# Hybrid decoder layer on one core: two seams rewritten, and divided products placed by what PE has just done

## The chip, the core and the metric

The kernel runs on one core of one Trainium2 chip. The metric is the device time of one execution in microseconds (us), lower is better. The kernel before took 1909.48 us, the median of three runs (1909.34 to 1909.83).

## The reference

One decoder layer over a residual stream h of 256 rows by 2048 columns, all in f32:

```python
h = h + 0.5 * rms_norm(swiglu_ffn(rms_norm(h, g1), w_gu, w_down), p1)      # FFN1, d_ff = 5632
u = rms_norm(h, g2);  z = u @ w_in                                           # 2048 x 5120
a, g, q, k, v = split(z, [1024, 2048, 3072, 4096])
conv = silu(layer_norm(causal_depthwise_conv31(a * sigmoid(g))))
attn = causal_attention(rope(q), rope(k), v)       # 8 heads of 128; one block of 256 holds the sequence
h = h + rms_norm(concat(conv, attn) @ w_out, p2)
c = cross_attention(rms_norm(h, g3), rms_norm(mem, gm))   # 4 heads of 128, mem is 256 x 2048
h = h + rms_norm(c @ w_o, p3)
h = h + 0.5 * rms_norm(swiglu_ffn(rms_norm(h, g4), w_gu2, w_down2), p4)     # FFN2
```

where `swiglu_ffn(x) = (silu(x @ gate) * (x @ up)) @ down`, and rms_norm divides a row by the root of its mean square and multiplies by a gain.

## The kernel before

**Products.** Every f32 operand is split in two f32r parts, hi and lo, and a product is the sum of hi·hi, hi·lo and lo·hi. A weight tile is 128 partitions x 1024 columns (512 KB). It is loaded on SP's DMA queue into one of four `raw` buffers; ACT makes its hi (L183 where the norm's gain is multiplied in, L181 where not), DVE its lo (L199, L197). Each tile then gives PE 24 products of 256 columns. In `proj_T` (L443: gate and up, input projection, q, k) the weights stand still and a tile of activations moves; in `proj` (L457: down, v, `w_out`, x_o) the weights move. Activations lie in `chunk` tiles (`ck` and `cf` in the rows) of 512 columns, results in eight PSUM banks (`ps`).

**Order of the work.** Tiles are numbered as PE takes them. FFN1: 22 groups of gate and up with 8 tiles each (0 to 175), then down in two halves of 44 tiles (176 to 263). A boundary of residual updates, transposes (L340) and splits follows, in which PE is given products for the memory's k and v. Mixing: groups of the GLU, q, k and v, then the attention and, on DVE and POOL, the convolution's taps and its layer norm, then `w_out`. Cross-attention: q, attention, x_o (its 192 products with two activation chunks as operands come in two parts, first rows t = 0, then t = 1). FFN2 is FFN1 again.

**What runs beside.** `Weights.ahead()` issues loads and splits some tiles ahead. `Background` holds the small work (norms, gates, taps, transposes) in lanes: `add` puts a piece in, `cut` ends what one tile may take, and `step()` runs once per tile. The rows x are wanted as transposed chunks, 4 of them, put among the weights at tiles `X_AT` of the first group. A norm is four pairs of squares, a root, a diagonal, a broadcast on PE (L406) and a copy.

**Divided products.** `HALVED = (0, 4, 8)` names products of a tile that are given to PE as two of 128 columns. Before, they stand at fixed tiles: `(g, u) in ((1, 1), (2, 1))` of gate and up, `(hf, n) in ((0, 1), (0, 5))` of down, and `u == 1` of each group that is transposed in mixing.

**The start and the seam.** `Weights.start()` (L125 to L148) loads the first x chunk and the first weight tile by halves, behind one load of small vectors (L261). The seam before FFN2 is written out by hand behind the products of x_o: the transposes of t = 0, squares, gains and hi/lo of t = 0, then the last square of t = 1, the root (L496), reciprocal (L498), update (L501), transposes (L340), hi (L348), lo (L351), and the products of FFN2.

Of the kernel before, what the change touches and what calls it, by code (L numbers as in the profile page):

```python
# [33 lines left out]
X_AT = [0, 1, 3, 5]  # L34
# [12 lines left out]
class Background:  # L47


    def __init__(self):  # L50
        self.lanes = [deque(), deque()]
        self.lane = 0
        self.dve = deque()
        self.pool = deque()
        self.rate = (STEP_DVE, STEP_ACT, STEP_POOL)
        self.credit = [0.0, 0.0, 0.0]

    def add(self, fn, dve=0.0, act=0.0, pool=0.0):
        self.lanes[self.lane].append((fn, dve, act, pool))
# [8 lines left out]
    def step(self):  # L68
        self.credit = [min(c + d, d) for c, d in zip(self.credit, self.rate)]
        for lane in self.lanes:  # L70
            while lane:
                p = lane.popleft()
                if p is None:
                    break
                p[0]()
                self.spend(*p[1:])
# [23 lines left out]
class Weights:  # L100
# [10 lines left out]
    def add(self, src, gains=(None,), key=None, rows=False, loads=1):  # L111
        self.entries.append((src, gains, key, rows, loads))

    def load(self, upto):
        while self.n_raw < min(upto + 1, len(self.entries)):
            t = self.pool.tile([P, 1024], F32, name="raw", bufs=RAW)
            src, loads = self.entries[self.n_raw][0], self.entries[self.n_raw][4]
            n = 1024 // loads
            for e in range(loads):
                self.nc.sync.dma_start(t[:, e * n:(e + 1) * n], src[:, e * n:(e + 1) * n])  # L120
            self.raw[self.n_raw] = t
            self.n_raw += 1

    def start(self):

        for i in range(2):
            self.raw[i] = self.pool.tile([P, 1024], F32, name="raw", bufs=RAW)
        for i, e in ((0, 0), (1, 0), (1, 1), (0, 1)):
            c = slice(e * 512, (e + 1) * 512)
            self.nc.sync.dma_start(self.raw[i][:, c], self.entries[i][0][:, c])  # L130
        key = self.entries[0][2]
        self.chunks[key] = c = self.chunk()
        self.hi[key], self.lo[key] = c[:, :, 0, :], c[:, :, 1, :]
        self.hi[1] = self.pool.tile([P, 1024], F32R, name="hi", bufs=HI)
        self.lo[1] = self.pool.tile([P, 1024], F32R, name="lo", bufs=LO)
        for i, e in ((0, 0), (1, 0), (1, 1), (0, 1)):
            k = i if i else key
            src, hi, g = list(self.parts(i, self.hi[k]))[e]
            lo = list(self.parts(i, self.lo[k]))[e][1]
            if g is None:  # L140
                self.nc.scalar.activation(hi, src, AF.Copy)
                self.nc.vector.tensor_tensor(lo, src, hi.bitcast(F32), ALU.subtract)
            else:
                self.nc.scalar.activation(hi, src, AF.Copy, scale=g)  # L144
# [3 lines left out]
        self.n_raw = self.n_hi = self.n_lo = 2  # L148

    def parts(self, i, whole):  # L150

        _, gains, _, rows, _ = self.entries[i]
# [12 lines left out]
    def split_hi(self, upto):  # L165
        while self.n_hi < min(upto + 1, len(self.entries)):
            i = self.n_hi
            self.load(i)
            _, _, key, rows, _ = self.entries[i]
# [58 lines left out]
def layer_kernel(ctx: ExitStack, tc: tile.TileContext, x, mem, eye, consts, smalls, post_g, xt, memt,  # L228
# [32 lines left out]
    nc.sync.dma_start(sm[:, 0:S_CW], smalls[:, 0:S_CW])  # L261
# [3 lines left out]
    ones = cp.tile([P, P], F32, name="ones")  # L265
    nc.vector.memset(ones, 1.0)
# [6 lines left out]
    def add_ffn(gu, down, gain, extra):  # L273
        for g in range(2 * NG):
            for u in range(8):
                extra(-1, 8 * g + u)
                W.add(gu[g, u], [gain + 2 * u, gain + 2 * u + 1], loads=2 if len(W.entries) == 1 else 1)
# [11 lines left out]
    def first_extra(hf, k):  # L289
        kv_extra(0, hf, k, KV_AT1)  # L290
        if hf == -1 and k in X_AT:
            c = X_AT.index(k)
            W.add(xt[c], [None] * (2 if c == 0 else 1), ("x", c), True, 2 if c == 0 else 1)
# [4 lines left out]
    add_ffn(f1_gu, f1_down, S_G1, first_extra)  # L298
# [18 lines left out]
    add_ffn(f2_gu, f2_down, S_G2, lambda hf, k: None)  # L317

    def step(mm, k):
        W.ahead()  # L320
        hi, lo = W.take()
        mm(k, hi, lo)
        bg.step()
# [29 lines left out]
    class Rows:  # L353
# [10 lines left out]
        def tr(self, t, c):  # L364
            if self.xT[c] is None:
                self.xT[c] = chunk()
            self.ps[t, c] = transposes(self.src(t, c))

# [52 lines left out]
        def queue_norm(self, done=0):  # L421
# [25 lines left out]
    def proj(pss, first, last, hi, lo, xk, t, n0=0, halved=()):  # L447
# [3 lines left out]
        for n, ps in enumerate(pss):  # L451
            for o in (0, 256):
# [11 lines left out]
    class Post:  # L464


        def __init__(self, row, factor):
# [4 lines left out]
            self.ssq = [scal(4) for _ in range(2)]  # L472
# [14 lines left out]
        def early(self, t):  # L487

            s1 = scal()
            nc.vector.reduce_sum(s1, self.ssq[t][:, 0:3], axis=AX.X)  # L490
# [3 lines left out]
        def rstd(self, t):  # L494
            s2 = scal()
            nc.scalar.activation(s2, self.ssq[t][:, 3:4], AF.Sqrt, bias=self.bias, scale=self.factor / D)  # L496
            self.rs[t] = scal()
            nc.vector.reciprocal(self.rs[t], s2)  # L498

# [4 lines left out]
    def down(nk, lhs, post, hook=None, tail=TAIL, keep=False, order=None):  # L504

        order = order or range(nk)
        for hf in range(2):
# [3 lines left out]
            def mm(n, hi, lo):  # L511
# [36 lines left out]
    def boundary(post, last, rows, fillers):  # L548
# [36 lines left out]
        queue_rest(post, rows)  # L585

    def queue_rest(post, rows, early=False):
# [5 lines left out]
        def turns(c):  # L593
            for t in range(1 if early else 0, 2):
                bg.add(lambda t=t: rows.tr(t, c))
# [48 lines left out]
    def gate_up(rows):  # L644
        hT = []
        for g in range(2 * NG):
            pss = [bank() for _ in range(2)]

            def mm(u, hi, lo):
                for e in range(2):  # L650
                    k = 2 * u + e
                    proj_T(regions_of(pss), k == 0, k == KT - 1, hi[:, e * 512:], lo[:, e * 512:], rows.x(k),
                           g == k == 0, HALVED if e == 0 and (g, u) in ((1, 1), (2, 1)) else ())

            for u in range(8):
                step(mm, u)
            if g % 2 == 0:
                hT.append(chunk())
            c = slice(2 * (g % 2), 2 * (g % 2) + 2)
            queue_gate(pss[0], pss[1], rows, hT[-1][:, c, 0, :], hT[-1][:, c, 1, :])  # L660
# [56 lines left out]
    nc.sync.dma_start(sm[:, S_CW:S_W], smalls[:, S_CW:S_W])  # L717
    for c in range(4):
# [11 lines left out]
    hT = gate_up(rows)  # L730
# [49 lines left out]
    def in_group(hook=None):  # L780
        pss = [bank() for _ in range(2)]

        def mm(u, hi, lo):
            for e in range(2):
                k = 2 * u + e
                proj_T(regions_of(pss), k == 0, k == KT - 1, hi[:, e * 512:], lo[:, e * 512:], rows.x(k), False,
                       HALVED if u == 1 and e == 0 else ())
# [122 lines left out]
    def queue_heads(heads):  # L910
        stages = [attn_stages(hh) for hh in heads]
        for n in range(len(stages) + 7):
            for i in range(len(stages)):
                if 0 <= n - i < 8:
                    fn, d, a = stages[i][n - i]
                    bg.add(fn, dve=d, act=a)
            bg.cut()

    def queue_ln():
# [62 lines left out]
        bg.add(means)  # L982
# [7 lines left out]
        bg.add(squares)  # L990
# [26 lines left out]
    def v_group(c, hook):  # L1017
# [3 lines left out]
        def mm(u, hi, lo):  # L1021
            for e in range(2):
                k = 2 * u + e
                for t in range(2):
                    proj([vps[t]], k == 0, k == KT - 1, hi[:, e * 512:], lo[:, e * 512:], rows.x(k), t)
# [46 lines left out]
    def mm_q(u, hi, lo):  # L1072
        for e in range(2):
            k = 2 * u + e
            proj_T(regions_of(qps), k == 0, k == KT - 1, hi[:, e * 512:], lo[:, e * 512:], rows.x(k))
# [38 lines left out]
    for n in range(XH + 4):  # L1114
        for i in range(XH):
            if 0 <= n - i < 5:
                fn, d, a = xs[i][n - i]
                bg.add(fn, dve=d, act=a)
# [81 lines left out]
    bg.add(lambda: rows.tr(1, 1))  # L1200
# [4 lines left out]
    hT = gate_up(rows)  # L1205
# [106 lines left out]
```

## Time and profile before

| | |
|---|---|
| median of three runs | 1909.48 us |
| the profiled execution's own time | 1908.69 us |
| its span | 1906.9 us |
| PE busy | 1885.5 us, 99% |
| DVE, ACT, POOL busy | 62%, 55%, 11% |
| read from memory | 365.61 MB, 193 GB/s over the span |

PE is the TensorE's matmuls, PEld its weight loads, DVE, ACT and POOL the vector, scalar and GpSimd engines, SP the queue that issues most transfers. The span is what the profiler saw, from the first instruction to the last; the execution's own time is 1.8 us longer. A matmul's end is modelled, so paces are read from starts: in rows of the form "start, busy, engine, line" the second number is the time from the first start to the last end of a run of like instructions. The share of 99% says that PE hardly ever waits; it says nothing on how fast it goes while busy.

### The profile page before, as it was taken

To read this page: it belongs to the slowest core of one execution; us is meant where nothing else is said; L and a number is where in the kernel's file an instruction comes from. 1 tells how busy PE (TensorE), PEld (TensorE's weight loads), DVE (VectorE), ACT (ScalarE), POOL (GpSimd) and SP (SyncE) were. 2 spreads that over 40 slices of the span, in tenths; PEclk is the share of its full clock that TensorE was granted. 3 is DMA by queue.
4 is the path that set the end of the run, shared out by engine and by line. 5 is a ranking of instruction groups with operands and counts; after the bars stand their busy time and mean duration, and the time that the engine had idled before them with its cause. 6 is when DMAs were issued, how large, how long until landed. Compare 5 with 4: busy or idle time off the path is not lost.

```text
span 1906.9 us, 39744 instructions
## 1 busy us (share of the span) xinstructions
PE 1885.5 (99%) x16436; PEld 1880.9 (99%) x16436; DVE 1182.6 (62%) x1611; ACT 1049.7 (55%) x1627; POOL 205.8 (11%) x182
## 2 busy tenths in 40 slices
PE   8999999999999999999999999999999999999998
PEld 8999999999999999999999999999999999999998
DVE  5656665666544457898886675666666666644444
ACT  6655555555444556687675575555555555533433
POOL 0000000000000000598420000000000000000000
PEclk9999999999999999999999999999999999999999
DMA  8556565555655775555555573555565555655554
GB/s 297 190 193 197 191 198 191 198 190 198 210 196 192 244 247 171 182 184 173 177 183 183 182 229 101 183 197 192 195 194 194 195 193 196 214 191 197 192 195 144
DMA packets 102133, 370.28 MB, mean 194 GB/s; under 512 B 11456, under 2 KB 11712, under 8 KB 101184
## 3 DMA queue, kind: packets, MB, share of 16 engines
q1 hardware_dynamic: 100944, 361.00, 57.2%
q10 hardware_dynamic: 1008, 6.75, 1.1%
q8 instruction: 128, 2.10, 0.5%
q14 instruction: 53, 0.43, 0.1%
HBM read 365.61 MB, written 2.10 MB: 193 GB/s over the span
## 4 chain that ended last, share of the span: by engine, by line
PE 95%; DMA 1%; DVE 1%; POOL 1%; ACT 1%; issue 0%; SPq 0%; DVEq 0%; POOLq 0%; ACTq 0%
PE ps L443 60%; PE ps L457 32%; POOL cv L778 1%; DMA raw<-in_f_gu_dram 1%; DMA raw<-in_f_down_dram 1%; PE ps L340 0%; PE ps L1133 0%; PE ps L1131 0%; PE ps L1132 0%; ACT hi L181 0%; DVE lo L197 0%; POOL cf L947 0%; PE ps L869 0%; PE ps L1153 0%; PE ps L1091 0%
## 5 line engine op out<-in xcount | busy, mean ns | idle before, releaser
L443 PE MATMUL ps<-ck,hi 128*128 128x256 f32 x6808 | 1166.7, 277 | 8.2 <-ACT hi L144 6.9
L443 PEld LDWEIGHTS ps<-ck,hi 128*128 128x128 f32 x6808 | 1027.3, 188 | 9.2 <-ACT hi L144 6.9
L443 PE MATMUL ps<-ck,lo 128*128 128x256 f32 x3404 | 938.9, 277 | 1.5 <-DVE lo L197 1.2
L199 DVE SCALAR_TENSOR_TENSOR lo<-raw,sm,hi 128x512 fp32r<-128x512 f32 x718 | 517.5, 762 | 356.7 <-issue 337.0
L183 ACT ACTIVATE hi<-raw,sm 128x512 fp32r<-128x512 f32 x718 | 479.7, 717 | 373.1 <-PE ps L443 231.1
L443 PEld LDWEIGHTS ps<-ck,lo 128*128 128x128 f32 x3404 | 638.2, 188 | 2.2 <-DVE lo L197 1.6
L457 PE MATMUL ps<-hi,ck 128*128 128x256 f32 x3596 | 616.4, 277 | 0.0
L197 DVE TENSOR_TENSOR lo<-raw,hi 128x1024 fp32r<-128x1024 f32 x296 | 373.1, 1261 | 288.4 <-PE ps L457 228.8
L457 PEld LDWEIGHTS ps<-hi,ck 128*128 128x128 f32 x3596 | 542.9, 188 | 0.4
L457 PE MATMUL ps<-lo,ck 128*128 128x256 f32 (+1 forms) x1798 | 496.6, 277 | 0.3 <-DVE lo L197 0.3
L181 ACT ACTIVATE hi<-raw 128x1024 fp32r<-128x1024 f32 x296 | 313.0, 1059 | 312.8 <-PE ps L457 251.5
L457 PEld LDWEIGHTS ps<-lo,ck 128*128 128x128 f32 x1798 | 337.1, 188 | 0.6 <-DVE lo L197 0.5
L629 POOL TENSOR_TENSOR tmp<-tmp,rb 128x512 f32<-128x512 f32 x44 | 57.9, 1316 | 1128.4 <-ACT tmp L628 1128.4
L778 POOL TENSOR_TENSOR cv<-cv,cf 128x255 f32<-128x255 f32 (+14 forms) x120 | 123.3, 1029 | 306.4 <-ACT cf L777 298.3
L777 ACT ACTIVATE cf<-yv,cf 128x255 f32<-128x255 f32 (+14 forms) x120 | 56.7, 490 | 25.7 <-POOL cv L778 25.4
L768 DVE SCALAR_TENSOR_TENSOR ps<-yv,cf,ps 128x254 f32<-128x254 f32 (+28 forms) x116 | 54.4, 469 | 2.4
L348 ACT ACTIVATE ck<-tmp 128x512 fp32r<-128x512 f32 x44 | 27.8, 632 | 46.1 <-DVE tmp L632 46.1
L345 ACT ACTIVATE tmp<-ps 128x512 f32<-128x512 f32 x32 | 19.1, 598 | 33.0 <-PE ps L457 28.5
L482 DVE TENSOR_TENSOR fg<-ps,cf 128x512 f32<-128x512 f32 x32 | 21.3, 685 | 15.8 <-ACT tmp L345 15.8
L625 DVE TENSOR_TENSOR tmp<-ps,rb 128x512 f32<-128x512 f32 x44 | 30.1, 685 | 0.1
L351 DVE TENSOR_TENSOR ck<-tmp,ck 128x512 fp32r<-128x512 f32 x44 | 30.1, 685 | 0.0
L632 DVE TENSOR_TENSOR tmp<-tmp,ps 128x512 f32<-128x512 f32 x44 | 29.6, 674 | 0.0
(132 smaller groups left out, 649.6 us busy)
## 6 DMA issues: line engine op xcount, KB each, us to landing
raw<-in_f_gu_dram SPq DMA_DIRECT2D x351, 512.0 KB, 4.2
raw<-in_f_down_dram SPq DMA_DIRECT2D x176, 512.0 KB, 4.2
raw<-in_w_in_dram SPq DMA_DIRECT2D x80, 512.0 KB, 3.3
raw<-in_w_out_dram SPq DMA_DIRECT2D x32, 512.0 KB, 3.5
cf<-in_post_g_dram ACTq DMA_DIRECT2D x4, 1024.0 KB, 6.5
raw<-in_x_k_dram SPq DMA_DIRECT2D x8, 512.0 KB, 4.5
raw<-in_x_q_dram SPq DMA_DIRECT2D x8, 512.0 KB, 4.0
raw<-in_x_o_dram SPq DMA_DIRECT2D x8, 512.0 KB, 4.3
```

Of the source, the lines that this page charges most:

```text
L181: self.nc.scalar.activation(dst, src, AF.Copy)
L183: self.nc.scalar.activation(dst, src, AF.Copy, scale=g)
L197: self.nc.vector.tensor_tensor(dst, src, hi.bitcast(F32), ALU.subtract)
L199: self.nc.vector.scalar_tensor_tensor(dst, src, g, hi.bitcast(F32), ALU.mult, ALU.subtract)
L351: nc.vector.tensor_tensor(lo, src, hi.bitcast(F32), ALU.subtract)
L443: nc.tensor.matmul(ps[:, o + a:o + a + w], (hi, hi, lo)[i][:, j * P:(j + 1) * P], xk[:, i % 2, a:a + w], start=first and o == 0 and i == 0 ...
L457: nc.tensor.matmul(ps[:, a:a + d], xs[i], w[:, c:c + d], start=first and a == 0 and i == 0, stop=last and i == 2, skip_group_check=True)
L625: nc.vector.tensor_tensor(two(box[0]), two(G), bc2(rows.rb), ALU.mult)
L629: nc.gpsimd.tensor_tensor(two(box[0]), two(box[0]), bc2(rows.rb), ALU.mult)
L768: nc.vector.scalar_tensor_tensor(o, yv[:, ct, :S - s], w, a[:, s:], ALU.mult, ALU.add)
L777: nc.scalar.activation(pr[:, :S - s], yv[:, ct, :S - s], AF.Copy, scale=w)
L778: nc.gpsimd.tensor_tensor(cv[:, ct, s:], cv[:, ct, s:], pr[:, :S - s], ALU.add)
```

## The change

- **Start.** The small vectors are loaded on ACT's queue. The first transfers are a quarter of the x chunk, half a weight tile, a quarter, half, two whole weight tiles and then the rest of the x chunk. Nine f32 products of a tile of ones with itself are given to PE first. The first three groups of gate and up of FFN1 run side by side (`gu_order`, `SIDE = 3`): for each u one tile of each of the three groups; `X_AT` moves with them. The loads of the residual rows are four cuts later.
- **Divided products.** `Background.settle()` decides for each tile. Pieces that give PE other work than these products are marked `pe=True`; when one has run, or at the start of a half of down, behind a boundary, or behind the seam, `mixed` is set. The next tile but a group's first (`k` not 0) is divided if `mixed` is set and no marked piece stands in the next five cuts of any lane. It now holds for v groups and q too, and x_o has one fixed divided product set.
- **Norms.** One more cut stands between the root and the diagonal of each norm, so that everything behind it comes a tile later.
- **The seam before FFN2.** The last bank of x_o is computed in two sides of 256 columns; the last square is done in two halves; the update, transposes, hi and lo of the first chunk of t = 1 go by halves, with ACT's other work behind them.

```diff
-X_AT = [0, 1, 3, 5]
+X_AT = [0, 4, 10, 16]
+SIDE = 3
...
+    def settle(self, ahead=5):
+        if not self.mixed:
+            return False
+        for lane in self.lanes:
+            n = 0
+            for p in lane:
+                n += p is None
+                if n >= ahead:
+                    break
+                if p is not None and p[4]:
+                    return False
+        self.mixed = False
+        return True
...
     def start(self):
-        for i, e in ((0, 0), (1, 0), (1, 1), (0, 1)):
-            c = slice(e * 512, (e + 1) * 512)
+        x0, w0 = (0, slice(0, 256), slice(0, 1)), (1, slice(0, 512), None)
+        x1, w1 = (0, slice(256, 512), slice(1, 2)), (1, slice(512, 1024), None)
+        x2 = (0, slice(512, 1024), slice(2, 4))
...
+        for p in (x0, w0, x1, w1):
+            fetch(*p)
+        self.n_raw = 2
+        self.load(3)
+        fetch(*x2)
+        for p in (x0, w0, x1, w1):
+            split(*p)
+        self.n_hi = self.n_lo = 2
+        self.split_lo(2)
+        split(*x2)
...
-    nc.sync.dma_start(sm[:, 0:S_CW], smalls[:, 0:S_CW])
+    nc.scalar.dma_start(sm[:, 0:S_CW], smalls[:, 0:S_CW])
+    ones = cp.tile([P, P], F32, name="ones")
+    nc.vector.memset(ones, 1.0)
+    wps = bank()
+    for _ in range(9):
+        nc.tensor.matmul(wps[:, 0:P], ones, ones, start=True, stop=True)
...
+    def gu_order(side):
+        return [(g, u) for u in range(8) for g in range(side)] + [(g, u) for g in range(side, 2 * NG) for u in range(8)]
...
     def step(mm, k):
         W.ahead()
         hi, lo = W.take()
+        halved[:] = HALVED if k and bg.settle() else ()
         mm(k, hi, lo)
+        halved[:] = ()
         bg.step()
...
             bg.add(self.rstd, dve=0.4, act=0.4)
+            bg.cut()
             bg.add(self.diag, dve=0.4)
             bg.cut()
-            bg.add(self.bcast)
+            bg.add(self.bcast, pe=True)
...
-                    at = HALVED if t == 0 and (hf, n) in ((0, 1), (0, 5)) else ()
-                    proj(pss[t], n == 0, n == nk - 1, hi, lo, lhs(order[n]), t, 0, at)
+                    proj(pss[t], n == 0, n == nk - 1, hi, lo, lhs(order[n]), t, 0, halved if t == 0 else ())
+            bg.mixed = True
...
-                           g == k == 0, HALVED if e == 0 and (g, u) in ((1, 1), (2, 1)) else ())
+                       u == 0 and g < side and (side > 1 or e == 0), halved if e == 0 else ())
...
+    for _ in range(4):
+        bg.cut()
     for c in range(4):
         for t in range(2):
             bg.add(lambda t=t, c=c: nc.sync.dma_start(h_rows(t, c), x[t * P:(t + 1) * P, c * 512:(c + 1) * 512]))
...
-            proj(ps0[2 * hf:2 * hf + 2], k == 0, k == XH - 1, *wo[4 * hf + k], oT[:, k], 0)
+            proj(ps0[2 * hf:2 * hf + 2], k == 0, k == XH - 1, *wo[4 * hf + k], oT[:, k], 0, 0,
+                 HALVED if (hf, k) == (0, 1) else ())
...
-        for k in range(XH):
-            proj([ps1[c]], k == 0, k == XH - 1, *wo[4 * (c // 2) + k], oT[:, k], 1, c % 2)
+        for sides in [(0, 256)] if c < 3 else [(0,), (256,)]:
+            for k in range(XH):
+                proj([ps1[c]], k == 0, k == XH - 1, *wo[4 * (c // 2) + k], oT[:, k], 1, c % 2, (), sides)
...
-    post.early(1)
-    for c in range(2):
-        rows.hi(0, c)
-        rows.lo(0, c)
-    post.square(1, 3, ps1[3])
+    post.square_half(1, 0, ps1[3])
+    post.early(1, 4)
+    post.square_half(1, 1, ps1[3])
     post.rstd(1)
-    post.update(1, 0)
+    rows.hi(0, 0)
+    for e in range(2):
+        post.update_half(1, 0, e)
+        rows.tr_half(1, 0, e)
+    rows.hi_half(1, 0, 0)
+    rows.lo_half(0, 0, 0)
+    rows.lo_half(1, 0, 0)
+    rows.hi_half(1, 0, 1)
+    rows.lo_half(0, 0, 1)
+    rows.lo_half(1, 0, 1)
+    rows.hi(0, 1)
     post.gain(1, 3, ps1[3])
-    rows.tr(1, 0)
-    rows.hi(1, 0)
-    rows.lo(1, 0)
+    rows.lo(0, 1)
     post.update(1, 1)
```

**The order of instructions at three places.** SP's queue from its first transfer, before:

```order
L261 DMA sm<-in_smalls_dram 128x80
L130 DMA raw<-in_xt_dram 128x512
L130 DMA raw<-in_f_gu_dram 128x512 x2
L130 DMA raw<-in_xt_dram 128x512
L120 DMA raw<-in_xt_dram 128x1024
L120 DMA raw<-in_f_gu_dram 128x1024 x2
L120 DMA raw<-in_xt_dram 128x1024
L120 DMA raw<-in_f_gu_dram 128x1024
L716 DMA ident<-in_eye_dram 128x128
```

The same stretch after (`in_xt` is x transposed, `in_f_gu` the weights of gate and up):

```order
L153 DMA raw<-in_xt_dram 128x256
L153 DMA raw<-in_f_gu_dram 128x512
L153 DMA raw<-in_xt_dram 128x256
L153 DMA raw<-in_f_gu_dram 128x512
L140 DMA raw<-in_f_gu_dram 128x1024 x2
L153 DMA raw<-in_xt_dram 128x512
L140 DMA raw<-in_f_gu_dram 128x1024
L140 DMA raw<-in_xt_dram 128x1024
L140 DMA raw<-in_f_gu_dram 128x1024
L797 DMA ident<-in_eye_dram 128x128
```

The small vectors are gone from the head of this queue, a quarter of x stands ahead of the first half tile of weights, and the second whole transfer of x comes behind three whole weight tiles rather than ahead of them. DVE at the seam before FFN2, before:

```order
L482 TENSOR_TENSOR fg<-ps,cf 128x512 x3
L490 TENSOR_REDUCE scal_14397<-scal_14099 128x1
L492 TENSOR_SCALAR scal_14399<-scal_14397 128x1
L351 TENSOR_TENSOR ck<-ps,ck 128x4x128 x2
L498 RECIPROCAL scal_14409<-scal_14407 128x1
L501 SCALAR_TENSOR_TENSOR h<-fg,scal_14409,h 128x512
L482 TENSOR_TENSOR fg<-ps,cf 128x512
L351 TENSOR_TENSOR ck<-ps,ck 128x4x128
L501 SCALAR_TENSOR_TENSOR h<-fg,scal_14409,h 128x512
```

And after (L482/L550 is the gain, L351/L399 the lo, L501/L575/L579 the update):

```order
L550 TENSOR_TENSOR fg<-ps,cf 128x512 x3
L562 TENSOR_REDUCE scal_14403<-scal_14100 128x1
L565 TENSOR_SCALAR scal_14405<-scal_14403 128x1
L571 RECIPROCAL scal_14411<-scal_14409 128x1
L575 SCALAR_TENSOR_TENSOR h<-fg,scal_14411,h 128x256 x2
L399 TENSOR_TENSOR ck<-ps,ck 128x2x128 x4
L550 TENSOR_TENSOR fg<-ps,cf 128x512
L399 TENSOR_TENSOR ck<-ps,ck 128x4x128
L579 SCALAR_TENSOR_TENSOR h<-fg,scal_14411,h 128x512
```

The two lo's of t = 0 stood ahead of the reciprocal and now stand behind the update, which has become two halves. PE from the end of the cross-attention to FFN2, before:

```order
L1104 MATMUL ps<-ident,cf 128x128 x4
L1153 MATMUL ps<-cf 128x256 x8
L457 MATMUL ps<-ck 128x256 x192
L340 MATMUL ps<-ident,h 128x128 x20
L443 MATMUL ps<-ck,hi 128x256 x8
```

And after:

```order
L1238 MATMUL ps<-cf 128x256 x8
L525 MATMUL ps<-ck 128x256 x12
L525 MATMUL ps<-ck 128x128 x2
L525 MATMUL ps<-ck 128x256 x3
L525 MATMUL ps<-ck 128x128 x2
L525 MATMUL ps<-ck 128x256 x3
L525 MATMUL ps<-ck 128x128 x2
L525 MATMUL ps<-ck 128x256 x171
L388 MATMUL ps<-ident,h 128x128 x16
L424 MATMUL ps<-ident,h 128x128 x4
```

Three of x_o's 192 products are now two each; the last four transposes have become two pairs (L424).

## Rows read from the trace of the kernel before

**Rows 1.** The page: busy us of an engine, share, instructions.

```profile
PE 1885.5 (99%) x16436; PEld 1880.9 (99%) x16436; DVE 1182.6 (62%) x1611; ACT 1049.7 (55%) x1627; POOL 205.8 (11%) x182
```

**Rows 2.** PE's waits: waiting line, releaser; total us, times, longest.

```profile
PE ps L443 <- ACT hi L144: 6.9, 1, 6.9
PE ps L340 <- DVE h L501: 1.8, 1, 1.8
PE ps L443 <- DVE lo L197: 1.2, 2, 1.0
```

**Rows 3.** The chain that ended last: start us, us, what.

```profile
52.90 438.49 PE ps L443 x3867
...
661.34 45.99 PE ps L457 x406
...
736.48 2.87 PE ps L443 x24
...
759.17 8.49 PE ps L443 x72
...
1147.37 23.03 PE ps L457 x192
```

**Rows 4.** Timeline of PE, a divided tile: start us, us, engine, line.

```profile
35.62 0.51 PE L443 MATMUL ps<-ck,hi 128*128 128x128 f32 x3
...
37.23 0.28 PE L443 MATMUL ps<-ck,lo 128*128 128x256 f32 x1
```

**Rows 5.** Timeline of PE, the first products and the stall at 20 us.

```profile
6.89 2.08 PE L443 MATMUL ps<-ck,hi 128*128 128x256 f32 x8 [6.89 <-ACT hi L144]
...
10.63 0.28 PE L443 MATMUL ps<-ck,lo 128*128 128x256 f32 x1
...
19.93 0.28 PE L443 MATMUL ps<-ck,lo 128*128 128x256 f32 x1
...
21.84 0.40 PE L443 MATMUL ps<-ck,hi 128*128 128x256 f32 x2
```

**Rows 6.** Windows: busy us of five engines; granted clock; DMA share; GB/s.

```profile
6.89:10.47 3.58, 3.58 (x16) 3.58 (x17) 2.71 (x4) 2.73 (x4) 0.00 (x0) 1.00 0.83 310
10.00:20.00 10.00, 10.00 (x84) 9.95 (x82) 6.27 (x8) 4.90 (x7) 0.00 (x0) 1.00 1.00 333
```

**Rows 7.** The chain of the first 60 us.

```profile
1.64 4.39 DMA raw<-in_f_gu_dram
...
6.12 0.73 ACT hi L144
...
13.33 6.62 DMA raw<-in_f_gu_dram
...
52.47 0.43 PE ps L406 x2
```

**Rows 8.** Timeline of SP's queue: the first issue.

```profile
0.74 0.38 SPq L261 DMA_DIRECT2D sm<-in_smalls_dram  x1
```

**Rows 9.** Timeline of the seam before FFN2.

```profile
1170.24 1.91 PE L340 MATMUL ps<-ident,h 128*128 128x128 f32 x16
...
1171.84 0.60 ACT L345 ACTIVATE tmp<-ps 128x512 f32<-128x512 f32 x1
...
1173.09 0.75 DVE L501 SCALAR_TENSOR_TENSOR h<-fg,scal,h 128x512 f32<-128x512 f32 x1
...
1173.99 0.63 PE L340 MATMUL ps<-ident,h 128*128 128x128 f32 x4 [1.85 <-DVE h L501]
...
1175.31 1.47 PE L443 MATMUL ps<-ck,hi 128*128 128x256 f32 x8 [0.69 <-ACT ck L348]
...
1176.61 0.63 PE L443 MATMUL ps<-ck,lo 128*128 128x256 f32 x4
```

**Rows 10.** The chain in mixing: where it leaves PE and comes back.

```profile
840.10 0.56 DVE tmp L801
...
869.68 1.48 DVE lo L197
```

More of the change, by code (lines that the diff above doesn't have):

```diff
@@ L109, in __init__, with add @@
         self.limit = None
-    def add(self, src, gains=(None,), key=None, rows=False, loads=1):
-        self.entries.append((src, gains, key, rows, loads))
+    def add(self, src, gains=(None,), key=None, rows=False):
+        self.entries.append((src, gains, key, rows))
     def load(self, upto):
@@ L116, in load @@
             t = self.pool.tile([P, 1024], F32, name="raw", bufs=RAW)
[L117 to L120, printed above, removed]
+            self.nc.sync.dma_start(t, self.entries[self.n_raw][0])
             self.raw[self.n_raw] = t
@@ L168, in split_hi @@
             self.load(i)
-            _, _, key, rows, _ = self.entries[i]
+            _, _, key, rows = self.entries[i]
             if rows:
@@ L271, in layer_kernel, with add_ffn @@
     W = Weights(nc, wp, chunk, sm)
[L273 to L277, printed above, removed]
+    def gu_order(side):
+        return [(g, u) for u in range(8) for g in range(side)] + [(g, u) for g in range(side, 2 * NG) for u in range(8)]
+    halved = []
+    def add_ffn(gu, down, gain, extra, side):
+        for n, (g, u) in enumerate(gu_order(side)):
+            extra(-1, n)
+            W.add(gu[g, u], [gain + 2 * u, gain + 2 * u + 1])
         for hf in range(2):
@@ L292, in first_extra @@
             c = X_AT.index(k)
-            W.add(xt[c], [None] * (2 if c == 0 else 1), ("x", c), True, 2 if c == 0 else 1)
+            W.add(xt[c], key=("x", c), rows=True)
         if hf == 1 and k in MEM_AT:
@@ L316, in layer_kernel @@
             W.add(x_o[o // 4, o % 4], key=("o", o))
[L317 removed]
+    add_ffn(f2_gu, f2_down, S_G2, lambda hf, k: None, 1)
     def step(mm, k):
@@ L367, in tr, with tr_half, hi_half, lo_half @@
             self.ps[t, c] = transposes(self.src(t, c))
+        def tr_half(self, t, c, e):
+            if self.xT[c] is None:
+                self.xT[c] = chunk()
+            if (t, c) not in self.ps:
+                self.ps[t, c] = bank().rearrange("p (k s) -> p k s", k=4)
+            for k in (2 * e, 2 * e + 1):
+                nc.tensor.transpose(self.ps[t, c][:, k], self.src(t, c)[:, k * P:(k + 1) * P], ident)
+        def hi_half(self, t, c, e):
+            k = slice(2 * e, 2 * e + 2)
+            make_hi(self.part(t, c, 0)[:, k], self.ps[t, c][:, k])
+        def lo_half(self, t, c, e):
+            k = slice(2 * e, 2 * e + 2)
+            make_lo(self.part(t, c, 1)[:, k], self.ps[t, c][:, k], self.part(t, c, 0)[:, k])
+            if e == 1:
+                self.ps.pop((t, c))
         def part(self, t, c, e):
@@ L445, in proj_T, with proj @@
                                  skip_group_check=True)
-    def proj(pss, first, last, hi, lo, xk, t, n0=0, halved=()):
+    def proj(pss, first, last, hi, lo, xk, t, n0=0, halved=(), sides=(0, 256)):
         xs = [xk[:, f, t * P:(t + 1) * P] for f in (0, 1, 0)]
@@ L451, in proj @@
         for n, ps in enumerate(pss):
-            for o in (0, 256):
+            for o in sides:
                 for i, w in enumerate((hi, hi, lo)):
@@ L471, in __init__ @@
             self.factor = factor
-            self.ssq = [scal(4) for _ in range(2)]
+            self.ssq = [scal(5) for _ in range(2)]
             self.fg = [None, None]
@@ L594, in turns @@
             for t in range(1 if early else 0, 2):
-                bg.add(lambda t=t: rows.tr(t, c))
+                bg.add(lambda t=t: rows.tr(t, c), pe=True)
         def parts(c):
@@ L642, in queue_gate, with gate_up, mm @@
         bg.cut()
-    def gate_up(rows):
+    def gate_up(rows, side):
         hT = []
[L646 to L652, printed above, removed]
-                           g == k == 0, HALVED if e == 0 and (g, u) in ((1, 1), (2, 1)) else ())
[L655 to L660, printed above, removed]
+        pss = {}
+        def mm(g, u, hi, lo):
+            for e in range(2):
+                k = 2 * u + e
+                proj_T(regions_of(pss[g]), k == 0, k == KT - 1, hi[:, e * 512:], lo[:, e * 512:], rows.x(k),
+                       u == 0 and g < side and (side > 1 or e == 0), halved if e == 0 else ())
+        for g, u in gu_order(side):
+            if u == 0:
+                pss[g] = [bank() for _ in range(2)]
+            step(lambda u, hi, lo, g=g: mm(g, u, hi, lo), u)
+            if u == 7:
+                if g % 2 == 0:
+                    hT.append(chunk())
+                c = slice(2 * (g % 2), 2 * (g % 2) + 2)
+                queue_gate(*pss.pop(g), rows, hT[-1][:, c, 0, :], hT[-1][:, c, 1, :])
         return hT
@@ L728, in ffn1_hook @@
             mem_prep()
-    hT = gate_up(rows)
+    hT = gate_up(rows, SIDE)
     post = Post(0, 4.0)
@@ L915, in queue_heads @@
                     fn, d, a = stages[i][n - i]
-                    bg.add(fn, dve=d, act=a)
+                    bg.add(fn, dve=d, act=a, pe=n - i in (0, 3, 5))
             bg.cut()
@@ L981, in queue_ln @@
         bg.cut()
-        bg.add(means)
+        bg.add(means, pe=True)
         bg.cut()
@@ L989, in queue_ln @@
         bg.cut()
-        bg.add(squares)
+        bg.add(squares, pe=True)
         bg.cut()
@@ L1024, in mm @@
                 for t in range(2):
-                    proj([vps[t]], k == 0, k == KT - 1, hi[:, e * 512:], lo[:, e * 512:], rows.x(k), t)
+                    proj([vps[t]], k == 0, k == KT - 1, hi[:, e * 512:], lo[:, e * 512:], rows.x(k), t, 0,
+                         [m - 6 * t for m in halved] if e == 0 else ())
         for u in range(8):
@@ L1117, in layer_kernel @@
                 fn, d, a = xs[i][n - i]
-                bg.add(fn, dve=d, act=a)
+                bg.add(fn, dve=d, act=a, pe=n - i in (0, 3))
         bg.cut()
@@ L1185, in layer_kernel @@
         post.gain(1, c, ps1[c])
-    post.early(1)
-    for c in range(2):
-        rows.hi(0, c)
-        rows.lo(0, c)
-    post.square(1, 3, ps1[3])
-    post.rstd(1)
-    post.update(1, 0)
+    post.square_half(1, 0, ps1[3])
+    post.early(1, 4)
+    post.square_half(1, 1, ps1[3])
+    post.rstd(1)
+    rows.hi(0, 0)
+    for e in range(2):
+        post.update_half(1, 0, e)
[7 more added lines that the diff above has]
+    rows.hi(0, 1)
     post.gain(1, 3, ps1[3])
-    rows.tr(1, 0)
-    rows.hi(1, 0)
-    rows.lo(1, 0)
+    rows.lo(0, 1)
     post.update(1, 1)
-    bg.add(lambda: rows.tr(1, 1))
+    bg.add(lambda: rows.tr(1, 1), pe=True)
     bg.cut()
@@ L1204, in layer_kernel @@
     queue_rest(post, rows, True)
-    hT = gate_up(rows)
+    bg.mixed = True
+    hT = gate_up(rows, 1)
     post = Post(3, 4.0)
```

56 lines of the change are left out of this document (36 added, 20 removed).

## The prediction

> **What bounds the kernel now.** First the busy shares: PE is busy for 99% of the span, no other engine comes near [rows 1]. Then PE's waits: they add up to little, a first wait of 6.9 us, one of 1.8 us before the second feed-forward, 1.2 us in the mixing stage [rows 2]. So the time is PE's, and what can be won is in three kinds of loss: the first 25 us, the seam before the second feed-forward, and the pace of the products themselves. For the pace, divide the length of a piece of the chain by its count [rows 3]: 438.49 us / 3867 = 113.4 ns per product of 256 columns in the long stretch of FFN1; 8.49 / 72 = 117.9 ns behind transposes in the mixing stage; 23.03 / 192 = 119.9 ns in the products with x_o. The same instruction runs at two paces: after other work on PE it often goes on at 118, for as long as nothing intervenes, and it is a product divided into halves that brings it back to 113.4. A tile of 24 products is 2.72 us at the fast pace; the slow one adds 24 x 4.5 ns = 0.108 us.
>
> **What one division costs.** From the first divided product at 35.62 us to 37.23 us there are 14 starts, 3 of them extra [rows 4]: 1.61 us where 11 products at 113.4 take 1.25. So a divided tile costs 0.36 us, and it pays only if the pace was slow and more than 0.36 / 0.108 = 3.4 tiles follow without a disturbance. After the broadcast of the memory's norm 406 products took 45.99 us, 113.3 each, without any division [rows 3]: in products with the weights as moving operand PE can come back by itself. By their own numbers many divisions of the kernel before buy nothing.
>
> **The head.** The first 17 products take from 6.89 to 10.63 us [rows 5], 3.74 us or 220 ns each, where 17 x 0.118 = 2.00: 1.74 us lost. The granted clock of that stretch is given as 1.00, 2.4 GHz [rows 6], but near the double of 118 ns looks like the lower level, 1.2 GHz; the engine had done nothing before. From 19.93 to 21.84 us four products take 1.91 us instead of 0.47 [rows 5]: 1.44 us lost, at the end of a weight transfer that took 6.62 us [rows 7] while the DMA engines were full, 333 GB/s at a share of 1.00 [rows 6].
> Changed: (a) nine f32 products of ones by ones run on PE while it would wait for the first transfer. A norm's broadcast of 256 f32 columns took 0.43 us [rows 7]; 128 columns at half the clock are as long, nine 3.8 us (an estimate), from about 1 us to about 5 us: as much as the engine had done before it rose, and over before the first real product. A wait of 1.85 us in the seam did not slow what followed, four products took 0.63 us with 0.28 for the last [rows 5, 9], so 0.117 a start; 1 us of idleness should not slow it either. I take the whole 1.74 us; the bounds are 0 and 1.74. The Trainium skill says the same of cause and danger (TensorE: Matmul & The Clock Gate, Part 1): the clock is low by default, activity raises it, and idleness lowers it again.
> (b) The chain to the first product is the first half tile of weights (issued at 1.64, 4.39 us), then ACT's 0.73 us [rows 7]. It now stands behind a quarter of x instead of the small vectors and half of x: issued about 0.45 us earlier (two issues stood ahead of it from 0.74 [rows 8] to 1.64, now one), and 128 KB less ahead of it, 0.39 us at 333 GB/s. Bounds 0 and 1.2; I take 0.7, so a first product at 6.2 us.
> (c) Three groups run side by side over the same x, so a column tile of x is wanted every 12 weight tiles' worth of products rather than every 4, and x's chunks, the residual rows (four steps later) and the weights no longer crowd into 10 to 40 us. PE eats a 512 KB tile in 2.83 us, 185 GB/s, against the 333 the queue gave. I see the 1.44 us gone; the bounds are 1.44 and a new wait of the same size. Where it would be: w3 may only be loaded when the first weight buffer is free, about 8.1 us, lands near 12.5 (the first half tile took 4.39 us among others [rows 7]) and is wanted at 6.2 + 3 x 2.83 = 14.7. The norm's broadcast, five tiles later, is still two tiles ahead of the first gate; that hides it.
> (d) Division at tile 3 and directly behind the broadcast, instead of tiles 9 and 17: 11 tiles at the slow pace become 3, 8 x 0.108 = 0.87, less what the cold products already covered: 0.8 us. The number of divisions is 2 in both.
> Head: 1.74 + 0.7 + 1.44 + 0.8 = 4.7 us; the ends of all four together are -0.6 and 5.2.
>
> **Where divisions go.** By the order, 18 before, 14 after: FFN1 gate and up 2 and 2 (counted above), its down half 2 and 3, the boundary to mixing 2 and 1, mixing 8 and 4, x_o 0 and 1, FFN2 gate and up 2 and 1, its down half 2 and 2. None of the four removed up to FFN1's boundary and in FFN2 stood in a slow stretch that lasted, so each counts +-0.36: down half +0.36, boundary -0.36, FFN2 -0.36. The one behind FFN1's last broadcast is a pure cost (113.3 there anyway).
> Mixing: two of the four fewer lie before 840 us and two behind. From 840.10 (DVE's gate, released by PE) the chain leaves PE, runs through ACT and POOL and comes back by DVE's lo at 869.68 [rows 10]; PE waits there twice, 1.2 us together by the waits [rows 2]. A PE that is 0.72 us faster behind 840 only waits that much longer. So -0.72 counts and -0.72 does not. The extra cut in the norm shifts the taps one tile later against the rope's copies on ACT and POOL: this can move that wait either way. Bounds: -3.2 (all four count and the waits go) and +1.8 (the waits double).
> x_o: the 120 ns pace. Those products have both operands in chunk tiles, and so have the kv fillers, which also run at 2.87 / 24 = 119.6 ns [rows 3]; so here I read 120 as the price of these operands and not as a leftover, and a division as 0.36 us lost. The other end is 7 tiles x 24 x 6.5 ns = 1.1 saved less 0.36, -0.7; I take +0.36, by the nearer row.
>
> **The seam before FFN2.** Last product of x_o, 16 transposes from 1170.24, then the chain: ACT's last square only at 1171.84 (it stood behind two hi's on ACT), update 1173.09 for 0.75, four transposes 1173.99, hi, first product 1175.31 [rows 9]. Now half of that square is done while the other half of the bank is computed, and the rest comes first on ACT: from about 1170.44 half of 0.60 and a bit, 0.4; then the 0.65 us that lay between that square's end (1172.44) and the update; then a half update, 0.42, so the first half is there at 1171.9, when the 16 transposes end (1171.98). Two transposes 0.4 with their latency (four took 0.63), half a hi 0.4 (behind a whole one PE waited 0.69): first product at about 1172.85, 2.45 us earlier. What is late next: DVE, with two half updates, four half lo's, a gain, a lo and the update of the second chunk in a row, is done near 1176.1, while PE wants that chunk's transposes at 1172.85 + 2.83 = 1175.7. PE then waits about 0.45. Net -2.0; bounds -1.2 and -2.8.
>
> **Sum.** -4.7 (head) + 0.36 - 0.36 - 0.72 (mixing) + 0.36 (x_o) - 2.0 (seam) - 0.36 = -7.4 us. The profiled execution took 1908.69 us (span 1906.9 and 1.8 around it), the median is 1909.48: 1901.3 on the one, **1902.1 us** on the other, which I forecast.
>
> **Rivals.**
> The warming products do nothing, or the clock falls back in the idle us behind them: 1.74 back, 1903.8. For it: no row shows PE idle after so short a warm phase. Against it: the 1.85 us in the seam.
> Mixing eats more: ACT, POOL and DVE are the bound behind 840, the waits grow by 1.75 and nothing of the 0.72 counts: 1904.6. For it: the chain there is not PE's [rows 10].
> Mixing's waits go, since the rope's copies now stand ahead of two taps more: 1899.6.
> x_o's division takes hold: -1.5 against my sum, 1900.6, if 120 ns is a leftover of the f32 products ahead as 118 is. The Trainium skill gives PE two independent read ports, so that loading weights takes nothing from the moving operand (TensorE: Matmul & The Clock Gate, Part 2), which speaks for this case; the 119.6 ns of the fillers speak against it.
> The first transfers come no earlier and a wait returns in tiles 1 to 4: 0.7 + 1.44 back, 1904.2.
> Slower: the new rule divides only behind known other work, not behind a stall. Should PE stall after the division at tile 20 (a late x chunk or a row load), it stays at 118 ns until the down half, tile 177, with nothing to bring it back: up to 155 x 0.108 = 17 us, 1919. It decides against the change when the stall comes before tile 108 (69 tiles eat the 7.4 us). Against it: in 52.90 to 491 us no stall is seen [rows 3], and the loads are lighter there than now.
>
> **Chances.** Forecast 0.50 (own range 1900.7 to 1903.5), warming fails 0.12, mixing eats 0.10, its waits go 0.09, x_o 0.08, transfers 0.07, slower 0.04. 0.2% is 3.8 us, what a measurement here can tell from none: faster means under 1905.7. Of mixing 0.03 and of transfers 0.02 lie above that: faster 0.91, same 0.05, slower 0.04. Range 1898.8 to 1906.0: it holds all but the slow case, and the far ends of mixing and transfers.
>
> **What would show it.** Right: first product near 6.2 us, no starts 220 ns apart among the products with weights, no wait near 20 us, 113.4 from tile 3; tile 24 begun about 4.7 us earlier; x_o still 120; FFN2 begun 2.4 us after its last transposes of t = 0 began or a little more, and a short wait for the second update; the mixing stage's waits still there and longer. Wrong: 118 ns between 75 and 485 us; x_o at 113; a first product later than 6.9.

## The result and the profile after

Over 22 runs the changed kernel took 1923.94 us in the median, the kernel before 1910.07. The ratio is 1.006, with an interval of 1.0049 to 1.0071: slower, where 1902.1 and a range of 1898.8 to 1906.0 had been forecast. (The ratio leaves the two longest runs out.) 3 runs lie at 1906.5 to 1909.5 us, 17 at 1922.1 to 1926.1, 2 at 1941.1 and 1941.7. The 22 runs of the kernel before lie between 1908.5 and 1911.5, in one group.

The trace that came with the result is of a run of the first group (1909.51 us, span 1907.7). The page's line on the engines, answering to [rows 1]:

```profile
PE 1892.2 (99%) x16442; PEld 1887.2 (99%) x16442; DVE 1180.6 (62%) x1615; ACT 1049.8 (55%) x1631; POOL 205.8 (11%) x182
```

PE is busy 6.7 us longer. The nine products at the start are 4.2 us of it (1.05 to 5.26 us); the rest is looked for in the pace, so the chain is read as in [rows 3] (start us, us, what):

```profile
12.39 7.83 DMA raw<-in_f_gu_dram
...
21.88 42.43 PE ps L511 x358
...
64.75 424.66 PE ps L511 x3747
489.41 172.24 PE ps L525 x1518
662.08 70.99 PE ps L525 x603
...
1148.69 23.34 PE ps L525 x195
...
1203.23 454.58 PE ps L511 x4011
```

358 products from 21.88 us take 118.5 ns each, 3747 of FFN1's gate and up 113.3, the last 603 of its down half 117.7, where the kernel before had 113.3 [rows 3]. A second execution of the same kernel (1924.45 us), same view:

```profile
64.43 441.28 PE ps L511 x3747
...
1218.95 454.58 PE ps L511 x4011
```

The 3747 products of FFN1 take 117.8 ns each here: 441.28 - 424.66 = 16.6 us, the whole distance between the first group and the second, and 118 ns between 75 and 485 us is what the prediction had named as a sign of being wrong. FFN2's are as before; a second stage of this kind, 4011 x 4.5 ns = 18 us, would make the third group; no trace shows a run of it.

Starts of the first product of a tile, read from PE's timelines (us; the difference to the kernel before in brackets). A tile is 24 products in PE's order; the products for the memory's k, four tiles at each boundary, are counted, those for its v are not.

| tile | before | after, 1909.51 | after, 1924.45 | divisions a tile later (below) |
|---|---|---|---|---|
| 0 | 6.89 | 6.24 (-0.65) | 5.51 (-1.38) | 6.87 (-0.03) |
| 24 | 77.78 | 75.81 (-1.98) | 75.90 (-1.89) | 75.60 (-2.19) |
| 176, down | 491.22 | 489.25 (-1.98) | 505.55 (+14.32) | 489.04 (-2.19) |
| 264, boundary | 732.58 | 732.90 (+0.32) | 749.12 (+16.53) | 730.61 (-1.97) |
| 320 | 894.90 | 892.86 (-2.04) | 908.63 (+13.72) | 890.70 (-4.20) |
| 392 | 1147.01 | 1148.34 (+1.33) | 1164.07 (+17.06) | 1144.63 (-2.38) |
| 400, FFN2 | 1175.31 | 1175.38 (+0.07) | 1191.11 (+15.80) | 1171.67 (-3.64) |
| 624 | 1789.25 | 1789.08 (-0.16) | 1804.81 (+15.56) | 1785.59 (-3.66) |

### The profile page after: what moved, and what is told of

Same layout as the page of the kernel before. It is cut to its first block, busy times and chain, and to the rows that moved or that the text cites. A ratio compares the mean times of both kernels' runs of the same rounds, so it can differ in the third digit from the quotient of the medians.

```text
span 1907.7 us, 39764 instructions
## 1 busy us (share of the span) xinstructions
PE 1892.2 (99%) x16442; PEld 1887.2 (99%) x16442; DVE 1180.6 (62%) x1615; ACT 1049.8 (55%) x1631; POOL 205.8 (11%) x182
## 4 chain that ended last, share of the span: by engine, by line
PE 95%; POOL 2%; issue 1%; DVE 1%; DMA 1%; ACT 1%; SPq 0%; DVEq 0%; POOLq 0%; ACTq 0%
PE ps L511 58%; PE ps L525 33%; POOL cv L861 2%; PE ps L388 0%; DMA raw<-in_f_gu_dram 0%; PE ps L1218 0%; PE ps L1216 0%; PE ps L1217 0%; DMA raw<-in_xt_dram 0%; ACT hi L219 0%; POOL cf L1030 0%; PE ps L981 0%; PE ps L952 0%; PE ps L1238 0%; PE ps L1176 0%
## 5 line engine op out<-in xcount | busy, mean ns | idle before, releaser
L525 PE MATMUL ps<-lo,ck 128*128 128x256 f32 x1800 | 498.0, 277 | 0.0
L393 ACT ACTIVATE tmp<-ps 128x512 f32<-128x512 f32 (+1 forms) x33 | 19.3, 585 | 35.6 <-PE ps L525 31.0
L550 DVE TENSOR_TENSOR fg<-ps,cf 128x512 f32<-128x512 f32 x32 | 21.3, 685 | 16.0 <-ACT tmp L393 15.9
L399 DVE TENSOR_TENSOR ck<-tmp,ck 128x512 fp32r<-128x512 f32 x44 | 30.1, 684 | 0.0
```

The source lines that it names most:

```text
L525: nc.tensor.matmul(ps[:, a:a + d], xs[i], w[:, c:c + d], start=first and a == 0 and i == 0, stop=last and i == 2, skip_group_check=True)
```

## The experiments

Theory 1: a division directly behind a norm's broadcast does not always take hold (PE goes on at 118 ns behind it); a tile later it does. Theory 2: it takes hold, and a late load throws PE back afterwards.

**The changed kernel again** (no edit).

> The changed kernel as it is, for more times and a second trace. Its times so far stand in three groups, near 1907, 1924 and 1941 us, 17 us apart; 156 tiles of gate and up at 118 instead of 113.4 ns are 156 x 0.108 = 16.8 us. Both theories expect most runs near 1924 and, if the trace is of such a run, a whole gate-and-up stage at 118 ns. Theory 1 (the divided tile directly behind a norm's broadcast takes hold only in some executions): 118 ns from the first whole tile behind that division on, with no gap. Theory 2 (it takes hold, and a late load throws PE back later, with no division left to mend it): 113.4 ns for some tiles, then a gap of over 0.2 us, then 118.

Measured: 1923.9 in the median of 6 (1922.61 to 1942.85). In its trace PE runs at 118 ns from the first whole tile behind the division at 64 us on; no gap lies between. That speaks against theory 2.

**Divisions one tile later.**

```diff
+        if self.mixed == 1:
+            self.mixed = 2
+            return False
         self.mixed = False
         return True
```

> The changed kernel with each division by the new rule one tile later, so 24 whole products stand between a broadcast and the division. Theory 1: all runs near 1907 us (1905 to 1909), gate and up of both feed-forwards at 113.4 ns, and also the end of FFN1's down half (661 to 735 us), which ran at 118 behind its division in the profiled run: 2 us less there, up to 1.5 us more for the tile's delay at 14 places. Theory 2: the loads are the same, so most runs stay near 1924.

Measured: 1905.11 in the median of 7 (1904.53 to 1905.93), ratio to the kernel before 0.9974 (0.9963 to 0.9984). The groups are gone. The chain:

```profile
64.42 424.78 PE ps L514 x3747
...
661.97 68.80 PE ps L528 x603
...
1199.50 454.70 PE ps L514 x4011
```

The end of the down half is 2.2 us shorter with the same 603 products. Theory 1 holds; the order of the loads is the same.

**The kernel before, its divisions directly behind the broadcasts.**

```diff
-HALVED if e == 0 and (g, u) in ((1, 1), (2, 1)) else ()
+HALVED if e == 0 and (g, u) in at else ()     # FFN1 ((1, 1), (1, 7)), FFN2 ((1, 0),)
```

> The kernel before, with the division that followed FFN1's broadcast two tiles later moved directly behind it, and FFN2's, one tile later, as well (its second one there left out); all else as before. Theory 1: a part of the runs, perhaps most, gains 17 us (1926) and some 35 (1944), the rest stay at 1909; in the trace a slow stage begins right behind the division. Theory 2: nothing but the division's place has changed and no load is later, so 1909 to 1910 in every run, 113.4 ns in both stages.

Measured: 1926.0 in the median of 6, one run at 1909.67, five at 1925.71 to 1926.97, none near 1944. The chain of one of the five, against 438.49 us in [rows 3]:

```profile
53.80 455.41 PE ps L443 x3867
...
1217.67 457.32 PE ps L443 x4035
```

A kernel without any other part of the change shows the same fault: 117.8 ns in FFN1, 113.3 in FFN2. Theory 2 falls.

**One whole product between broadcast and first half.**

```diff
-HALVED = (0, 4, 8)
+HALVED = (1, 5, 9)
```

> The changed kernel with the second, sixth and tenth product of a divided tile divided instead of the first, fifth and ninth: one whole product stands between the broadcast and the first half. Reading 1a (only the very first product behind the f32 broadcast, with its 246 ns before the next start, spoils the division): every run near 1907 us. Reading 1b (PE must have settled at its slow pace for longer than one product before halves bring it back): the groups at 1907, 1924 and 1941 remain, most runs near 1924.

Measured: 1916.46 to 1919.1 in all 5 runs, 1916.83 in the median: neither number. Its chain:

```profile
64.19 424.67 PE ps L511 x3747
488.87 176.87 PE ps L525 x1518
...
1206.52 454.60 PE ps L511 x4011
1661.11 245.19 PE ps L525 x2118
```

Reading 1a holds for gate and up, 113.3 ns in every stage. But at the start of each down these three products do not mend the pace: 176.87 against 172.24 us and 245.19 against 240.33 for the same work, 9.5 us in all. PE goes on at 118 ns through the first half, tiles 178 to 220, and comes back with the division at the start of the second, tile 221; behind the broadcast of the memory's norm, tile 239, one whole product between was not enough. Why the same three products work at one place and not at another is not shown.

**Only the nine products at the start, on the kernel before.**

> The kernel before with only the nine f32 products of ones at the start. If what I forecast of them holds alone: the first 17 products at 118 instead of 220 ns, 1.7 us less, 1907.8. Rival: PE then reaches the weight tile that lands at 19.95 us 1.7 us sooner and waits that much longer for it, so tile 8 begins as before and the time stays within 0.3 us of 1909.5. Second rival: the clock falls back before the first product, 220 ns as before.

Measured: 1912.83 in the median of 11, ratio 1.0011 (1.0003 to 1.002): slower. PE's timeline, of the same form as [rows 5]:

```profile
7.28 1.76 PE L446 MATMUL ps<-ck,hi 128*128 128x256 f32 x8 [2.42 <-ACT hi L144]
```

Its window, of the same form as [rows 6] (the granted clock is the third number from the end):

```profile
7.28:10.90 3.62, 3.62 (x18) 3.62 (x19) 2.77 (x4) 2.77 (x4) 0.00 (x0) 0.56 0.80 301
```

PE waits 2.42 us between the last of the nine and the first product with weights (the first transfer landed 0.4 us later than in the trace of before). The first three products still follow each other at 118 and 138 ns, from the fourth on they come 213 ns apart, and the granted clock of the stretch is 0.56: most of it at 1.2 GHz. So the second rival holds here, from the fourth product on. In the first trace of the changed kernel the wait was 0.98 us, and the products came at 118; with divisions a tile later 1.61 us, and the first 17 came at 213:

```profile
6.87 2.07 PE L514 MATMUL ps<-ck,hi 128*128 128x256 f32 x8 [1.61 <-ACT hi L175]
```

The whole difference does not lie at the start, the only place that was edited. This trace is 4.1 us longer than that of the kernel before: 0.4 by the first product, 1.8 in FFN1's down half, where the 624 products behind the last broadcast took 73.25 us, 117.4 each, so that PE does not always come back by itself there, as it had in [rows 3]; 0.6 in mixing; and 1.4 at the seam before FFN2. Why all 11 runs lie above 1911 us is not shown.

**Thirteen products at the start, x_o whole.**

```diff
-for _ in range(9):
+for _ in range(13):
...
-                 HALVED if (hf, k) == (0, 1) else ())
+                 ())
```

> The kernel with divisions one tile later, 13 instead of 9 f32 products at the start (they end near 5.5 instead of 5.0 us), and x_o's three products whole again. If PE stays warm, the first 17 products with weights run at 118 ns instead of 213, 1.7 us less, and x_o gives 0.3: 1903.1. Rival: the weight tile that landed at 20.2 us in the changed kernel stops PE near 20.5 us again, as there (1.2 us), right behind the division of tile 5 (19.94 us), and PE goes on at 118 ns until the broadcast near 64 us, 15 tiles x 0.108 = 1.6 us: then nothing is won, 1904.8 to 1906.

Measured: 1904.37 in the median of 8 (1903.6 to 1907.54), 0.9971 (0.9961 to 0.9981): between the two, and not clear of the 0.9974 without them. No gap is left at the start: the first 17 products come at 118 ns, and x_o's 192 take 23.05 us, as before. PE then waits 0.5 us at 17.5 us for a weight tile; tile 8 begins 2.1 us earlier than without, tile 400 only 1.35. Most of the rest went in mixing: 1.1 us between tiles 320 and 328.

**Small loads later.**

```diff
-    nc.sync.dma_start(ident, eye)
-    nc.sync.dma_start(sm[:, S_CW:S_W], smalls[:, S_CW:S_W])
     for _ in range(4):
         bg.cut()
+    bg.add(lambda: nc.sync.dma_start(ident, eye))
+    bg.add(lambda: nc.sync.dma_start(sm[:, S_CW:S_W], smalls[:, S_CW:S_W]))
```

> As the kernel with 13 products, and the loads of the identity and of the second part of the small vectors (rows of 512 and 1088 bytes, issued at 11.4 and 11.9 us) moved behind the four cuts, ahead of the residual rows. If those small packets made the weight tile issued at 12.39 us take 7.8 us, it lands a microsecond or more sooner, the stall near 20.5 us goes and the time is 1.5 to 3 us under that of the kernel with 13 products. If the stall is the bandwidth of all transfers together (330 GB/s), the two are within 0.4 us: the moved loads are only 200 KB, 0.6 us.

Measured: 1904.68 in the median of 11 (1904.17 to 1907.3), within 0.4 us of the kernel with 13 products: moving the small loads buys nothing. In its trace PE waits near 17.5 us in the middle of the divided tile 4, the halves behind the wait do not take hold, and 384 products from 17.85 to 63.3 us come at 118 ns. In the trace of the kernel with 13 products the wait of 0.5 us stood at the same place of the same tile, and PE went on at 113.3.

**No extra cut in the norms.**

```diff
             bg.add(self.rstd, dve=0.4, act=0.4)
-            bg.cut()
             bg.add(self.diag, dve=0.4)
```

> The kernel with divisions one tile later, without the extra cut in each norm. The new wait of 1.0 us at the cross-attention's q products (for a lo of DVE) comes of the norm's broadcast being a tile later: without the cut it goes, -1.2 us there. The other reading is that DVE's queue makes that wait wherever the norm stands: same time. In mixing the cut may have helped (1.2 us were won between tiles 264 and 304, which I put down to four divisions fewer): if it was the cut, up to 1.2 us come back.

Measured: 1906.08 in the median of 11 (1904.94 to 1907.32), 1 us more than with the cut; as ratios, 0.9978 (0.9969 to 0.9987) against 0.9974, the two are not told apart, so the stages of the traces decide. Its waits in mixing, against 1.2 us in [rows 2] and 0.4 with the cut:

```profile
PE ps L513 <- DVE lo L238: 2.8, 2, 1.7
```

The wait in cross-attention goes (0.7 us between tiles 384 and 392). In mixing the 1.2 us of tiles 264 to 304 stay, so those were the divisions; between 304 and 320 2.2 us are lost, so there it was the cut that had won.

**All that had paid, two divisions less.** Divisions one tile later, thirteen products, x_o whole, no division at the start of the second halves of down, the head's division at tile 8 instead of 4.

> The kernel with 13 products at the start and divisions one tile later, with two divided tiles less (the second halves of both downs, where PE is at 113.3 ns already: 0.39 us each by the traces) and the head's division some five tiles later, behind the stall near 18 us, so that it can't be spoiled by it. If a division costs 0.36 to 0.39 us wherever it stands and mends only a slow pace: 1904.4 - 0.8 - (0 to 1.2 for the runs whose head stayed slow) + 0.5 = 1903 to 1904, and every run within 1 us of the others. If the second halves need their division after all, their 1000 products at 118 ns add 4.6 us each.

Measured: 1903.67 in the median of 5 (1902.61 to 1904.66), 0.9963 (0.9949 to 0.9977): the lowest median of all, though its interval overlaps that of the kernel with 13 products, and the runs lie 2 us apart, not 1. The second halves needed no division: PE runs at 113.3 ns there without.

## Why the prediction was wrong

The step that failed is (d) of the head, and the sentence that it rests on: "it is a product divided into halves that brings it back". Every division behind a norm's broadcast in the kernel before stood one tile or more later; I carried the rule to a place that no row showed. (The trace of before has a division directly behind the attention's f32 products, tile 333, and PE goes on at 113.3 ns there: it would have spoken for the wrong step.) Directly behind the broadcast of FFN1's norm they mostly fail to take hold: of 28 executions of the changed kernel 3 lie near 1907 us, all others one or two steps of 17 us higher, and in the traced one of these the 3747 products behind it run 4.5 ns longer each. The last rival priced this end, PE at 118 until the down half, at 17 us and gave it 0.04; only its trigger was wrong: no stall came behind the division.

The other terms, from the first trace's starts:

- **Head**, -4.7 forecast, -1.98 measured. The first product came 0.65 earlier (0.7 forecast), but that near hit is luck: in the second trace of the same kernel it came 1.38 earlier, and with divisions a tile later, behind the same first transfers, 0.03. The products at 118 instead of 220 ns gave their 1.7 us in this trace; in the second one the first seven still came at 213. The stall did not go: 1.2 us at 20.5 us, 1.44 before, since PE is 2.9 us ahead at tile 4 and meets a transfer that is not earlier (the weight tile issued at 12.39 us took 7.83 and landed at 20.22; before, one landed at 19.95 [rows 7]). And behind that stall, which came after the division at tile 3, PE ran at 118 ns up to the broadcast at 64 us: the rival's mechanism, in the small.
- **FFN1's down half**, +0.36 forecast, +2.30 measured. The division behind the broadcast was to cost its 0.36 and did (0.41); but it also kept PE at 118 ns, 0.85 us for every 8 tiles, where PE had come back by itself.
- **Boundary and mixing**, -1.08 forecast. Up to tile 304 -1.35, in four steps of 0.33 to 0.34, a division each: the price was right, the count not. I had put two of mixing's four fewer ahead of 840 us; three of them lie there (tiles 285, 293 and 301), and the fourth, at tile 309, soon after. Up to tile 320 another -1.01: 0.34 for that fourth, the rest by shorter waits for DVE's lo, 0.4 us instead of 1.2 [rows 2], which is the extra cut's doing (without it they are 2.8). I had left its sign open. Then +2.12 went again up to tile 384, of it 1.4 in `w_out`: the new rule divides tile 358, where PE was at 113.3 ns, and PE then goes on at 118 until the next division at tile 365. Two divided tiles at 0.40 and six tiles at 0.11. This is the failed step once more: the last f32 products of the attention begin at 1016.93 us, the first half at 1017.07. With the division a tile later PE stays at 113.3.
- **Cross-attention**, nothing forecast, +1.25. The products for the memory's v wait for a lo of DVE; 0.7 us of it goes without the extra cut, which makes the norm's broadcast come a tile later. I had thought of the cut in mixing only. PE's waits after:

```profile
PE ps L1218 <- DVE lo L235: 1.0, 1, 1.0
```

- **x_o**, +0.36 forecast, +0.31 measured (23.34 against 23.03 us): 120 ns with and without the division.
- **Seam**, -2.0 forecast, -1.6 measured (-1.26 with x_o's +0.31). The timeline, against [rows 9]:

```profile
1171.86 1.91 PE L388 MATMUL ps<-ident,h 128*128 128x128 f32 x16
...
1172.06 0.38 ACT L393 ACTIVATE tmp<-ps 128x256 f32<-128x256 f32 x1 [2.19 <-PE ps L525]
...
1172.43 0.38 ACT L393 ACTIVATE tmp<-ps 128x256 f32<-128x256 f32 x1
...
1173.53 0.88 DVE L575 SCALAR_TENSOR_TENSOR h<-fg,scal,h 128x256 f32<-128x256 f32 x2
1174.16 0.74 PE L424 MATMUL ps<-ident,h 128*128 128x128 f32 x4 [0.40 <-DVE h L575]
1175.38 1.21 PE L511 MATMUL ps<-ck,hi 128*128 128x256 f32 x8 [0.47 <-ACT ck L396]
```

The first update starts 1.67 us behind the first transpose instead of 2.85, and the first product 3.52 instead of 5.07. I had taken half a square off the path; both halves came after the transposes began (1172.06 and 1172.43): by the profile the first, too, was released only by PE's last products. The wait for the second update is 0.19 us, not 0.45.
- **FFN2**, -0.36 forecast, -0.23 measured up to tile 624. The tail, from the last product's start to the end, took 1.2 us more in this trace and 0.2 more in the second one; why stays open.

## What to carry to other kernels

A pace that a trick restores is a state: before a trick is moved, look in the trace for a place of the new kind, and give a price to its failing over all that follows, not to its own instructions. A run's trace may be of a rare group, so read the list of times ahead of it. And a step that is made earlier only pays up to the next transfer, which does not move with it.

## What was not expected of the hardware

The same 128x256 products go at 113.3 or 117.8 ns for a whole stage of 4000, with a granted clock of 1.00 in either (100 to 480 us of the two traces of the changed kernel); what sets which it is, was not found. Of the three traces with a division directly behind the broadcast FFN1's failed in two, and FFN2's, of the same form, in none; why they differ stays open. It is not the norms' broadcasts alone: the changed kernel also divides three tiles of mixing directly behind other f32 products, and in its two traces tile 358 fails twice, tile 345 once and tile 334 never. And in the trace of the kernel with the small loads later the first four tiles run at 113.3 ns with no division ahead of them.

In the trace of the kernel with only the nine products the clock was up, fell and rose again: granted 1.00 from 4 to 7.28 us, 0.56 from 7.28 to 10.9, 1.00 from 11.2 to 15. Ahead of the fall PE had waited 2.42 us and done three products. It happened at the seam too: the same waits of 1.85 and 0.69 us as in the kernel before [rows 9] were followed by 13 products 213 ns apart at a granted clock of 0.50, 1.37 us lost. So the wait that the prediction held against this rival did no harm in one trace and did in another. The Trainium skill (TensorE: Matmul & The Clock Gate, Part 1) says that idleness lowers the clock again; this trace agrees at both places. The other traces with nine products can't be sorted by the wait ahead of the first product with weights: after 0.60 and 0.98 us the products came at 118 ns, after 1.10 and 1.61 us the first 17 came at 213, and after 0.25 us the first seven. Their rows give the granted clock as 1.00 even where the products come at 213 ns, so whether it had risen and fallen or not yet risen is not shown.
